# The second mixer's HGRN2 f and q projections move into the seven-product stage, with rope computed in PSUM and a new order around it

## The chip, the cores and the metric

The kernel runs on one core of one Trainium2 chip. What counts is the device time of one execution in microseconds (us). The same outputs are computed before and after; a run of the kernel before and one of the changed kernel can be compared on the same chip.

The engines are named as the profile names them: PE is TensorE (matmuls; PEld is its weight load), DVE is VectorE, ACT is ScalarE, POOL is GpSimd, SP is SyncE, whose queue issues every DMA of this kernel, in order. Matmuls write to PSUM, 8 banks of 128 x 512 float32 values here. DVE and ACT read PSUM and SBUF; POOL works on SBUF alone.

## The reference

A decoder trunk of two layers over 1024 tokens of width 1024. Layer 0 has another mixer (gated DeltaNet and short convolutions), which the change doesn't touch. Layer 1 has the mixer below, and each layer ends with a SwiGLU feed-forward network. Of the mixer's input projection, `hq` and `hf` are 4 heads of 128 columns each (HGRN2), `hi` and `hg` the values and gates of these heads, `sq`, `sk` and `sv` the queries, keys and values of 3 patterns x 4 heads of windowed attention.

```python
D_MODEL, SEQ, DEPTH, BATCH = 1024, 1024, 2, 1
SWA_PATTERNS = ((128, 1), (512, 4), (2048, 16))
...
def rope(x, pos):
    ...
    return jnp.concatenate([x1 * cos - x2 * sin, x1 * sin + x2 * cos], axis=-1).astype(x.dtype)
...
def hgrn2_recurrence(q, k, v, log_f):
    '''S_t = diag(f_t) S_{t-1} + k_t v_t^T with k_t = 1 - f_t, o_t = S_t^T q_t, chunkwise.
    q, k, log_f: (B, T, H, dk); v: (B, T, H, dv).'''
...
def mixer_cd(h, w_in, lower_bound, norm_g, w_out):
    ...
    hq, hf, hi, hg, sq, sk, sv = split_cols(h @ w_in, CD_SPLITS)
    lb = lower_bound.astype(f32)
    hf = hf.astype(f32)
    f_gate = lb + (1.0 - lb) * jax.nn.sigmoid(hf)
    log_f = jnp.log(f_gate)
    k_in = (1.0 - lb) * jax.nn.sigmoid(-hf)
    ...
    o_c = hgrn2_recurrence(hgrn_heads(jax.nn.silu(hq), HG_DK), hgrn_heads(k_in, HG_DK),
                           hgrn_heads(hi, HG_DV), hgrn_heads(log_f, HG_DK))
    o_c = (rms_norm(o_c, norm_g) * jax.nn.sigmoid(hgrn_heads(hg, HG_DV).astype(f32))).reshape(b, t, HG_VW)
    ...
    sq = rope(sq.reshape(b, t, n_pat, SWA_HEADS, SWA_DH), pos)
    sk = rope(sk.reshape(b, t, n_pat, SWA_HEADS, SWA_DH), pos)
    ...
    for p, (window, dilation) in enumerate(SWA_PATTERNS):
        o_p, lse_p = dilated_window_attention(sq[:, :, p], sk[:, :, p], sv[:, :, p], window, dilation)
        outs.append(o_p)
        lses.append(lse_p)
    wts = jax.nn.softmax(jnp.stack(lses, axis=-1), axis=-1)
    o_d = jnp.einsum('bthpd,bthp->bthd', jnp.stack(outs, axis=3), wts).reshape(b, t, SWA_HEADS * SWA_DH)
    return jnp.concatenate([o_c.astype(h.dtype), o_d.astype(h.dtype)], axis=-1) @ w_out
```

## The kernel before

Every matmul with a weight is done three times: weights and activations are split into a high part that the fast matmul format holds exactly and a low rest (`split`, lines 102 and 103: a cast on ACT, then a subtraction on DVE), and `mm3` (lines 127 to 129) adds high x high, high x low and low x high into one PSUM bank.

The second mixer's projections run in two stages.

The seven-product stage is the class `Local`, a subclass of the feed-forward network's `Up`. It handles two 128-column weight blocks at once, a pair `f` ("g" and "u"). The activations are four blocks (two halves of the tokens x two halves of the 1024 input channels), `b11`, `b21`, `b12`, `b22`, and the two weight blocks have two halves each. The four output blocks come from seven products of 4 x 3 matmuls instead of eight: p1, p2, p5, p6, p7 and the two that `end21` and `end12` add. The weights are combined first (`sums`, `sums_late` on POOL) and split in four parts: `part_a` (a11 and a12), `part_b` (s2 and s1, of the combined tile `ws`), `part_c` (s3 and a22) and `part_d` (s4, half a tile). The activations' combinations t1 to t4 are made once, in `turn`, which also works on the pairs 0 to 2; `pair` (line 862) does pair `f` and finishes pair `f - 1`. PE's order within `pair` is p1, p2, end21 of the pair before, end12 of the pair before, p6, p5, p7. Before the change the stage has 12 pairs: the queries and keys of pattern 1, then 2, then 0 (`PATTERNS`), 4 heads each.

All 12 get rope (line 766). A finished block lies in SBUF (`c`, `gt`, `u`) or, for one of four, in the PSUM bank `psu`. ACT copies its two 64-row halves, exchanged, to `sw` (lines 774 and 775), POOL multiplies `sw` by the sine table, DVE multiplies the block by the cosine table (line 779), and a later call adds the two into `z` (line 787), which is stored to DRAM (`qk`). The order on PE, DVE, ACT, POOL and SP in this stage is the order of the code (`manual_schedule`): each engine works its list from the top and waits where something isn't ready.

The rest of the mixer is `mixer_cd`. Here a framework's scheduler orders the instructions by priority, and each engine again works a fixed list. The projections of HGRN2's f and q (`hgrn_fq`, 2 weights x 2 halves x 8 x 3 matmuls for a head), the values (`hgrn_v`, `swa_v`) and the gates (`hgrn_gates`) run on PE one after another, and after each piece `tick` adds credit for two interleaved programs: the chain of 8 recurrence units (`hgrn`, 4 heads x 2 halves: exponentials, a reciprocal, a logarithm, a scan, seven levels of decayed blocks, state update, norm) and the attention of 12 heads (`Attend`). DVE splits the weights and does most of the two programs' elementwise work. What attention is left over at the end runs alone. Then `out_proj` loads the 8 finished blocks of `cat` and projects them.

The order of the projections is written out by hand at the end of `mixer_cd`: f and q of head 0 with the values of heads 0 and 1, the values of pattern 1, f and q of heads 1 and 2, the values of heads 2 and 3, the values of patterns 2 and 0, f and q of head 3, the gates. Attention of a pattern may start after its values.

PSUM is three groups of banks: `psu` (3), `psm` (3), `psg` (2). The weight ring has 2 raw tiles (and a spare one in `Local`) and 4 split ones.

Of the kernel before, what the change touches and what calls it, by code (L numbers as in the profile page):

```python
# [9 lines left out]
F32 = mybir.dt.float32  # L10
# [8 lines left out]
P = 128  # L19
T_LEN = 1024  # L20
# [11 lines left out]
PATTERNS = (1, 2, 0)  # L32
# [23 lines left out]
def hybrid_trunk_kernel(ctx: ExitStack, tc: tile.TileContext, x_t, w_all, w_down, w_ba, vecs, c_f, c_i, c_rope, out):  # L56
# [686 lines left out]
    class Local(Up):  # L743

        def __init__(self, left):
            self.left, self.n = left, 0
            self.qk = [dr.tile([2, P, T_LEN], F32, name=f"qk{f}") for f in range(12)]
            self.b12 = dr.tile([P, KH, HT], F32, name="b12")
            self.units = {f: {} for f in range(13)}
# [4 lines left out]
        def source(self, kind, f):  # L754
            p, h = PATTERNS[f // 4], f % 4
            return w_all[W_AT["cd", (16 if kind == "g" else 28) + p * 4 + h]]
# [8 lines left out]
        def block(self, name="c"):  # L765
            return self.right.tile([P, HT], F32, tag="c", name=name, bufs=3)

        def rope(self, f, i, half, c, src=None):

            src = c if src is None else src  # L770
            r = (None, 4, 16)[PATTERNS[f // 4]]
            t = slice(half * HT, (half + 1) * HT)
            sw = self.right.tile([P, HT], F32, tag="sw", name="sw", bufs=2)
            S.copy(sw[0:64], src[64:128])
            S.copy(sw[64:128], src[0:64])  # L775
            G.tensor_tensor(sw, sw, self.table[:, 1, t], op=MULT)  # L776
            self.flush()
            c = self.block() if c is None else c
            V.tensor_tensor(c, src, self.table[:, 0, t], op=MULT)

            def add():
                z = self.right.tile([P, HT], F32, tag="z", name="z", bufs=3)
                a, b, d = c, sw, z
                if r:
                    a, b = (y.rearrange("p (i r) -> p i r", r=r) for y in (a, b))
                    d = d.rearrange("p (r i) -> p i r", r=r)
                V.tensor_tensor(d, a, b, op=ADD)
                self.stores.append(lambda: dma(self.qk[f][i, :, t], z))

            self.adds.append(add)  # L790
# [7 lines left out]
        def rope11(self, f):  # L798
            self.rope(f, 0, 0, self.g1.pop(f))

        def rope22(self, f):
            self.rope(f, 1, 1, self.c22.pop(f))

        def add22(self, f):
            c = self.c22[f] = self.block()
            S.copy(c, self.x[f])  # L806
            V.tensor_tensor(c, c, self.z[f], op=ADD)
# [1744 lines left out]
```

## Time and profile before

| | us |
|---|---|
| median of 3 runs | 2614.49 |
| fastest and slowest of the 3 | 2611.93, 2616.2 |
| the profiled execution | 2614.26 |
| its span, first to last instruction | 2612.5 |

The table of the page's first part gives each engine's busy time as a share of the span. A matmul's record is longer (390 ns for 512 columns) than the distance to the next one (about 227 ns), since matmuls are pipelined: a stretch counts as busy even where the next matmul starts late by less than the difference, and the waits are better read from the view of waits and from the times at which matmuls start. In the view of waits each row names the waiting group, what it waited for, the sum in us, how often, and the longest. In the view of stretches the columns are the stretch, its length, the busy time of PE, PEld, DVE, ACT and POOL with their instruction counts, the granted TensorE clock, the DMA engines' share and GB/s.

The stretches that matter lie between about 1130 us (the last matmul of layer 0's down projection) and 1882 us (PE dense again in the output projection of the second mixer).

### The profile page before, as it was taken

The page shows a single profiled execution, that of the slowest core. Times are in us where ns is not written, and L with a number is a line of the kernel's source. Part 1 is how long each engine was busy: PE and PEld are TensorE (multiplying, and loading weights), DVE is VectorE, ACT ScalarE, POOL GpSimd, SP SyncE. Part 2 cuts the span into 40 slices and gives each one's busy share as a digit, 9 for nine tenths or more (in the row PEclk, how much of TensorE's full clock was granted, in tenths as well). Part 3 has the DMA queues.
Part 4 walks back from the last instruction along what each step waited for, and adds up shares of the span by engine and source line. Part 5 has one row for each costly group of instructions (what it writes and reads, how often), then busy time and mean ns, then how long its engine had stood idle before and what let it go on. Part 6 is the DMA issues. An engine that isn't in the chain of part 4 may idle for free. (4 is left out here: it accounts for less than half of the span.)

```text
span 2612.5 us, 37301 instructions
## 1 busy us (share of the span) xinstructions
PE 2539.2 (97%) x14005; PEld 2100.0 (80%) x14005; DVE 1742.7 (67%) x2877; ACT 1045.3 (40%) x1727; POOL 629.0 (24%) x541
## 2 busy tenths in 40 slices
PE   9999999999999999998999999999699999999998
PEld 7888888888888888876777879888587888888887
DVE  8887786775656665489777576558667665566554
ACT  5432113443333444344445354455444333334442
POOL 0111121342423200135553000000024433331001
PEclk9999999999999999998999999999899999999999
DMA  4435447235565797523324234464562455668853
GB/s 158 150 117 186 126 153 266 85 121 174 177 210 202 237 305 248 169 85 109 101 97 150 83 121 98 122 175 154 161 234 73 162 170 196 206 202 291 278 179 125
DMA packets 271957, 434.70 MB, mean 166 GB/s; under 512 B 48128, under 2 KB 136736, under 8 KB 271520
## 3 DMA queue, kind: packets, MB, share of 16 engines
q1 hardware_dynamic: 271776, 432.32, 50.6%
q8 instruction: 110, 1.80, 0.3%
q14 instruction: 71, 0.58, 0.1%
HBM read 296.35 MB, written 135.87 MB: 165 GB/s over the span
## 5 line engine op out<-in xcount | busy, mean ns | idle before, releaser
L103 DVE TENSOR_TENSOR w<-raw,w 128x1024 fp32r<-128x1024 f32 (+1 forms) x319 | 383.4, 1204 | 135.7 <-ACT w L102 135.0
L102 ACT CAST w<-raw 128x1024 fp32r<-128x1024 f32 (+1 forms) x319 | 306.8, 963 | 284.3 <-PE psu L129 143.2
L127 PE MATMUL psu<-hnh,w 128*128 128x512 f32 x880 | 352.2, 400 | 5.3 <-ACT w L102 5.3
L129 PE MATMUL psu<-hnh,w 128*128 128x512 f32 x880 | 345.9, 393 | 3.1 <-DVE w L103 3.0
L128 PE MATMUL psu<-hnl,w 128*128 128x512 f32 x880 | 344.8, 392 | 0.0
L188 POOL TENSOR_TENSOR acc<-acc,sq 128x512 f32<-128x512 f32 x52 | 77.2, 1485 | 525.2 <-ACT sq L184 459.6
L129 PEld LDWEIGHTS psu<-hnh,w 128*128 128x128 f32 x880 | 166.0, 189 | 41.7 <-DVE w L103 6.8
L127 PEld LDWEIGHTS psu<-hnh,w 128*128 128x128 f32 x880 | 166.4, 189 | 40.2 <-ACT w L102 6.1
L128 PEld LDWEIGHTS psu<-hnl,w 128*128 128x128 f32 x880 | 166.6, 189 | 33.0
L326 POOL TENSOR_TENSOR ws<-raw 128x512 f32<-128x512 f32 x50 | 69.7, 1395 | 370.6 <-DMA raw<-in_dram 226.5
L103 DVE TENSOR_TENSOR w<-ws,w 128x1024 fp32r<-128x1024 f32 x47 | 62.1, 1322 | 126.6 <-ACT w L102 126.6
L103 DVE TENSOR_TENSOR hidq<-hr,hidq 128x1024 fp32r<-128x1024 f32 x72 | 82.0, 1140 | 76.5 <-ACT hidq L102 76.1
L127 PE MATMUL psu<-t4h,w 128*128 128x512 f32 x224 | 90.9, 406 | 21.3 <-ACT c L806 20.8
L102 ACT CAST hidq<-hr 128x1024 fp32r<-128x1024 f32 x72 | 70.3, 980 | 101.3 <-DMA hr<-ts 61.2
L127 PE MATMUL psm<-hidq,w 128*128 128x512 f32 (+1 forms) x275 | 106.1, 386 | 0.0
L128 PE MATMUL psm<-hidq,w 128*128 128x512 f32 (+1 forms) x275 | 105.8, 385 | 0.0
L129 PE MATMUL psm<-hidq,w 128*128 128x512 f32 (+1 forms) x275 | 105.8, 385 | 0.0
L776 POOL TENSOR_TENSOR sw<-sw,rope 128x512 f32<-128x512 f32 x48 | 73.3, 1536 | 102.7 <-ACT sw L775 88.5
L417 POOL TENSOR_TENSOR hid<-hid,c 128x512 f32<-128x512 f32 x44 | 62.5, 1421 | 127.5 <-ACT hid L416 127.4
L128 PE MATMUL psu<-t4l,w 128*128 128x512 f32 x224 | 89.5, 400 | 0.0
L129 PE MATMUL psu<-t4h,w 128*128 128x512 f32 x224 | 89.2, 398 | 0.0
L127 PE MATMUL psu<-t3h,w 128*128 128x512 f32 x224 | 87.3, 390 | 0.0
(533 smaller groups left out, 6643.0 us busy)
## 6 DMA issues: line engine op xcount, KB each, us to landing
raw<-in_dram SPq DMA_DIRECT2D x227, 512.0 KB, 4.1
sd<-in_dram SPq DMA_DIRECT2D x44, 512.0 KB, 3.7
hid<-hid SPq DMA_DIRECT2D x88, 256.0 KB, 2.7
sd<-sd SPq DMA_DIRECT2D x44, 512.0 KB, 3.2
hr<-ts SPq DMA_DIRECT2D x40, 512.0 KB, 4.4
raw<-sd SPq DMA_DIRECT2D x40, 512.0 KB, 4.7
hd<-h SPq DMA_DIRECT2D x48, 256.0 KB, 2.2
h<-hd SPq DMA_DIRECT2D x48, 256.0 KB, 5.9
```

Of the source, the lines that this page charges most:

```text
L102: S.copy(hi, src)
L103: eng.tensor_tensor(lo, src, hi.bitcast(F32), op=SUB)
L127: T.matmul(o, lh, rh, start=first and i == 0, stop=False, **kw)
L128: T.matmul(o, lh, rl, start=False, stop=False, **kw)
L129: T.matmul(o, ll, rh, start=False, stop=last and i == n - 1, **kw)
L188: (eng or G).tensor_tensor(a, a, q, op=ADD)
L326: G.tensor_tensor(s[:, HT:], b[:, :HT], b[:, HT:], op=ADD)
L417: G.tensor_tensor(h, h, self.c22.pop(f), op=MULT)
L776: G.tensor_tensor(sw, sw, self.table[:, 1, t], op=MULT)
```

## The change

The number of pairs in `Local` goes from 12 to 16: HGRN2's f and q of head h become a pair (`PAIRS`, key `(None, h)`), ahead of the queries and keys of patterns 1, 2, 0. These four are not turned by rope; their blocks are stored to DRAM as they are, and `hgrn_fq` loads b and q of a unit from there, one unit ahead. The clamp and the silu, which read PSUM before, read SBUF now.

For the turned pairs the finished block now lies in PSUM in all four cases: `add11` adds into the bank of p2, `add12` into the bank of p5, `add22` into a new `psm` bank, and rope's multiplication by the cosine writes back to the same bank. `sw` has 3 buffers instead of 2.

The order within `pair` changes: `copy22` (the copy that reads `x[f - 1]`) is issued ahead of `part_b`; `part_b` and `sums_late` of a pair move from the end of the pair before to its beginning; `part_c` moves behind `end21`. The first weights of the stage are split in `early`, which runs outside the hand-written order, so that the scheduler may place it beside the down projection before, and the pool `hx` of layer 0's feed-forward network stays open for it.

In `mixer_cd` the values of pattern 1 and 2 follow the values of heads 0 and 1, then the values of heads 2 and 3, of pattern 0, and the gates; `tick` gives more credit per piece (2.1 and 1.7 instead of 1.75 and 1.25), caps both, and attention takes credit only while there is something to do. The output projection of this layer takes the blocks in the order 0, 1, 2, 4, 5, 6, 3, 7 (before: 4, 5, 6, 7, 0, 1, 2, 3); 0 to 3 are HGRN2's heads and 4 to 7 attention's.

```diff
-PATTERNS = (1, 2, 0)
+PAIRS = [(None, h) for h in range(4)] + [(p, h) for p in (1, 2, 0) for h in range(4)]
...
         def source(self, kind, f):
-            p, h = PATTERNS[f // 4], f % 4
-            return w_all[W_AT["cd", (16 if kind == "g" else 28) + p * 4 + h]]
+            p, h = PAIRS[f]
+            base = (4, 0) if p is None else (16 + p * 4, 28 + p * 4)
+            return w_all[W_AT["cd", base["gu".index(kind)] + h]]
...
+        def out(self, f, i, half, tile):
+            d = self.qk[PAIRS[f]][i, :, half * HT:(half + 1) * HT]
+            self.stores.append(lambda: dma(d, tile))
...
+        def turned(self, f):
+            return PAIRS[f][0] is not None
+
+        def rope(self, f, i, half, src):
...
+            sw = self.right.tile([P, HT], F32, tag="sw", name="sw", bufs=3)
+            S.copy(sw[0:64], src[64:128])
+            S.copy(sw[64:128], src[0:64])
+            G.tensor_tensor(sw, sw, self.table[:, 1, t], op=MULT)
+            self.flush()
+            V.tensor_tensor(src, src, self.table[:, 0, t], op=MULT)
+
+            def add():
+                z = self.right.tile([P, HT], F32, tag="z", name="z", bufs=3)
+                a, b, d = src, sw, z
...
+                V.tensor_tensor(d, a, b, op=ADD)
+                self.out(f, i, half, z)
...
+        def copy22(self, f):
+            c = self.c22[f] = self.right.tile([P, HT], F32, tag="c", name="c", bufs=2)
+            S.copy(c, self.x[f])
+
+        def add22(self, f):
+            c = self.c22.pop(f)
+            if self.turned(f):
+                b = self.c22[f] = psm()
+                V.tensor_tensor(b, c, self.z[f], op=ADD)
+            else:
+                V.tensor_tensor(c, c, self.z[f], op=ADD)
+                self.out(f, 1, 1, c)
...
+        def add11(self, f):
+            g, y = self.g1[f], self.y[f]
+            if self.turned(f):
+                V.tensor_tensor(y, y, g, op=ADD)
+            else:
+                V.tensor_tensor(g, g, self.y.pop(f), op=ADD)
+                self.out(f, 0, 0, g)
...
         def rope21(self, f):
             x = self.x.pop(f)
-            self.rope(f, 1, 0, None, x)
+            if self.turned(f):
+                self.rope(f, 1, 0, x)
+            else:
+                z = self.right.tile([P, HT], F32, tag="z", name="z", bufs=3)
+                S.copy(z, x)
+                self.out(f, 1, 0, z)
+                self.flush()
...
         def add12(self, f):
-            h = self.u2[f]
-            V.tensor_tensor(h, h, self.z.pop(f), op=ADD)
+            h, z = self.u2.pop(f), self.z[f]
+            if self.turned(f):
+                V.tensor_tensor(z, z, h, op=ADD)
...
         def pair(self, f, last, b11, b21, b22, t1, t2, t3, t4):
             n = f + 1
             self.p1(f, b11)
-            self.add22(f - 1)
+            self.copy22(f - 1)
             if not last:
                 an = self.raw("g", n, n % 3 == 1)
...
-            self.part_c(f, self.b)
-            self.rope22(f - 1)
+            self.add22(f - 1)
+            self.part_b(f, self.s)
+            self.sums_late(self.a, self.b, self.s)
             self.p2(f, b21, psm())
             g = self.snap(f)
-            if f in (3, 4):
-                self.rope11(2) if f == 3 else self.rope12(1)
+            self.rope22(f - 1)
             self.end21(f - 1, t4)
-            self.add11(f, g)
+            self.add11(f)
+            self.part_c(f, self.b)
             self.rope11(f)
             self.end12(f - 1, b22)
             self.rope21(f - 1)
...
             self.add12(f - 1)
             if not last:
                 self.part_a(n, an)
-            self.rope12(f - 1)
             self.p5(f, t1, psg())
-            if f == 3:
-                self.rope12(0)
+            self.rope12(f - 1)
             if not last:
-                s = self.sums(an, bn)
-                self.part_b(n, s)
-                self.sums_late(an, bn, s)
+                self.s = self.sums(an, bn)
...
+        def early(self, hx):
...
+            u0, g0 = (ring.tile([P, DM], F32, tag="raw", name="raw", bufs=2) for _ in range(2))
+            dma(g0, self.source("g", 0))
...
+            self.part_a(0, g0)
+            self.part_a(1, ga)
...
+            self.part_a(2, w2)
+            s = self.sums(g0, u0)
...
-            def hgrn_fq(h, w, tick, halves=range(NH)):
...
+            def hgrn_fq(h, half):
+                b, q = raws[h, half] = hl("b", bufs=2), hl("q", bufs=2)
+                for i, z in enumerate((b, q)):
+                    dma(z, qkd[None, h][i, :, half * HT:(half + 1) * HT])
 
             def hgrn(h, half, states):
-                b, q = raws[h, half]
+                if half + h == 0:
+                    hgrn_fq(0, 0)
+                b, q = raws.pop((h, half))
                 kk = hl("kk", bufs=2)
 
-                t = hl("t", bufs=1)
+                V.tensor_scalar(b, b, -44.0, None, op0=MAX)
+                t = hl("t", bufs=2)
                 S.activation(t, b, AF.Exp, scale=-1.0)
+                th = hl("t", bufs=2)
+                S.activation(th, q, AF.Tanh, scale=0.5)
+                V.scalar_tensor_tensor(q, th, 1.0, q, op0=ADD, op1=MULT)
+                if h * 2 + half < 7:
+                    hgrn_fq(*divmod(h * 2 + half + 1, 2))
...
-                credit[0] = min(credit[0] + 1.75 * cost, 3.0)
-                credit[1] += 1.25 * cost
-                while credit[0] >= 1 and have_c[0] * 2 > done_c[0]:
+                credit[0] = min(credit[0] + 2.1 * cost, 3.0)
+                credit[1] = min(credit[1] + 1.7 * cost, 3.0)
+                while credit[0] >= 1 and have_v[0] * 4 > done_c[0]:
...
-                while credit[1] >= 1:
+                while credit[1] >= 1 and (wanted or heads or busy[0]):
...
-            wv = hgrn_vw(0)
-            for half in range(NH):
-                hgrn_fq(0, wf, tick, (half,))
-                hgrn_v(0, wv, tick, range(half * 4, half * 4 + 4))
-                have_c[0] = have_v[0] = 1
+            hgrn_v(0, wv, tick, range(4))
+            have_v[0] = 1
+            hgrn_v(0, wv, tick, range(4, 8))
             swa_v(1, tick)
             attend(1)
-            fq(1)
-            fq(2)
+            swa_v(2, tick)
+            attend(2)
             hgrn_v(1, hgrn_vw(1), tick)
             have_v[0] = 2
-            swa_v(2, tick)
-            attend(2)
             swa_v(0, tick)
             attend(0)
-            fq(3)
             hgrn_gates(tick)
...
-                             (4, 5, 6, 7, 0, 1, 2, 3), half, hp)
+                             ((4, 5, 6, 7, 0, 1, 2, 3), (0, 1, 2, 4, 5, 6, 3, 7))[layer], half, hp)
```

174 lines of the change are left out of this document (74 added, 100 removed).

## The prediction

> **What bounds the kernel now.** I read the page's engine shares first, then a table of stretches cut at the stage's borders, then PE's rows in order of time at these borders, then what stands ahead of the waits.
>
> ```profile
> span 2612.5 us, 37301 instructions
> PE 2539.2 (97%) x14005; PEld 2100.0 (80%) x14005; DVE 1742.7 (67%) x2877; ACT 1045.3 (40%) x1727; POOL 629.0 (24%) x541
> ```
>
> PE is busy for 97% of the span, so time can come off in two ways: fewer matmuls, or PE waiting less. How far apart matmuls start when nothing is late shows in two rows with 63 matmuls of 512 columns from the one to the other: 14.30 / 63 = 0.227 us. The other rows are the stages' borders and waits.
>
> ```profile
> 1115.22 0.40 PE L129 MATMUL psu<-hidq,w 128*128 128x512 f32 x1
> 1129.52 0.39 PE L129 MATMUL psu<-hidq,w 128*128 128x512 f32 x1
> 1134.04 0.80 PE L127 MATMUL psu<-hnh,w 128*128 128x512 f32 x1 [4.13 <-ACT w L102]
> 1205.13 0.80 PE L127 MATMUL psu<-t4h,w 128*128 128x512 f32 x1 [7.63 <-ACT c L806]
> 1206.14 0.63 PE L129 MATMUL psu<-t4h,w 128*128 128x512 f32 x1
> 1206.57 0.63 PE L127 MATMUL psu<-t4h,w 128*128 128x512 f32 x1
> 1339.65 0.50 PE L127 MATMUL psu<-t4h,w 128*128 128x512 f32 x1 [1.44 <-ACT c L806]
> 1360.17 0.50 PE L127 MATMUL psu<-t4h,w 128*128 128x512 f32 x1 [1.10 <-ACT c L806]
> 1405.32 0.39 PE L128 MATMUL psu<-hnl,w 128*128 128x512 f32 x1
> 1755.31 0.48 PE L127 MATMUL psu<-hnh,w 128*128 128x512 f32 x1
> ```
>
> The seven-product stage runs from 1129.75 (0.227 behind the last row of the down projection) to 1405.32, where its last product has just ended: 275.6 us, less 0.9 for four matmuls of head 0's f that stand among them, 274.7. Its work is 12 pairs x 7 x 12 matmuls x 0.227 = 228.8 us. So 45.9 us are lost there, 3.8 a pair, and a pair costs 22.9 us. Outside the stage a pair of projections is 8 x 12 matmuls, 21.8 us. As it ran, the stage saved nothing over the plain form.
>
> ```profile
> PE psu L127 <- ACT c L806: 20.8, 9, 7.6
> PE psu L129 <- DVE w L103: 2.8, 5, 1.1
> PE psu L127 <- ACT w L102: 1.2, 1, 1.2
> ```
>
> The waits between 1180 and 1412 are nearly all one: `end21` waits for the copy `c` that `add22` makes, nine times, once for each pair 3 to 11. Behind the long ones PE is slow as well: after the 7.63 us wait matmuls start 0.43 us apart (1206.14 and 1206.57).
>
> ```profile
> 1129.70:1187.00 57.30, 51.48 (x229) 40.72 (x229) 53.03 (x51) 28.84 (x36) 23.22 (x11) 0.94 0.24 85
> 1405.50:1755.00 349.50, 343.81 (x3219) 294.71 (x3219) 211.05 (x546) 165.99 (x372) 21.36 (x40) 1.00 0.43 123
> 1755.00:1882.00 127.00, 105.52 (x993) 88.11 (x993) 101.20 (x327) 60.40 (x149) 6.77 (x11) 0.92 0.48 146
> 1200.00:1225.00 25.00, 19.68 (x74) 15.78 (x75) 22.09 (x21) 12.86 (x21) 11.94 (x9) 0.80 0.37 124
> 1339.65:1360.17 20.52, 19.43 (x84) 15.61 (x84) 14.99 (x16) 10.00 (x16) 12.43 (x9) 1.00 0.31 103
> 1550.00:1575.00 25.00, 22.21 (x332) 19.05 (x332) 20.94 (x62) 15.15 (x33) 2.52 (x6) 1.00 0.23 76
> 1775.00:1800.00 25.00, 24.45 (x140) 21.05 (x139) 21.17 (x68) 14.82 (x34) 1.74 (x4) 1.00 0.60 185
> 1338.07 1.04 ACT L102 CAST w<-ws 128x1024 fp32r<-128x1024 f32 x1 [4.96 <-POOL ws L327]
> 1339.02 0.58 ACT L806 COPY c<-psu 128x512 f32<-128x512 f32 x1
> ```
>
> The reader is to see three things. In the first pairs DVE is full (22.09 of 25 us from 1200 on, the clock at 0.80). In a late pair (1339.65 to 1360.17) no engine is: DVE 14.99, ACT 10.00, POOL 12.43 of 20.52. There the wait is one of order: the last two rows show ACT standing 4.96 us for POOL's `ws`, then casting it, and only then making the copy that PE waits for. And in the rest (1405.5 to 1755) PE is covered, 343.81 of 349.50, with DVE at 60%.
>
> **The change part by part.** *Matmuls.* Four heads of f and q leave the rest with 4 x 96 = 384 matmuls, of which 380 lie behind 1405.32: 86.3 us. They come back as 4 x 84: the stage's work becomes 16 x 84 x 0.227 = 305.1 us. On counts alone that is 48 matmuls, 10.9 us.
>
> *The stage's waits.* `copy22` now stands ahead of the cast of `ws`, and needs only p7 of the pair before, while `end21` comes two products (5.4 us) later. So the wait for `c` should go. What is late next? I lay a turned pair out on 19.07 us (84 x 0.227), with 2.72 us a product (12 x 0.227), 1.38 for an operation on POOL (12.43 / 9, above) and the two ACT rows just read; the positions are estimates from these. POOL's `sums` end about 2 us into the pair, the cast and subtraction of `part_b` by 4.5; p6, the first to need it, starts at 10.9. `sums_late` ends at about 5.5, `part_c` by 8; p7 starts at 16.3. Each has 6 us to spare. `part_a` is split by about 16.7 for the next p1 at 19.07: the smallest margin, 2 us.
>
> *DVE in a pair.* That only holds if DVE keeps up.
>
> ```profile
> L103 DVE TENSOR_TENSOR w<-raw,w 128x1024 fp32r<-128x1024 f32 x21 | 31.2, 1490 | 0.4 <-ACT w L102 0.4
> L103 DVE TENSOR_TENSOR w<-ws,w 128x1024 fp32r<-128x1024 f32 x9 | 11.5, 1275 | 28.9 <-ACT w L102 28.9
> L103 DVE TENSOR_TENSOR w<-raw,w 128x512 fp32r<-128x512 f32 x10 | 6.8, 676 | 0.0
> L787 DVE TENSOR_TENSOR z<-c,sw 128x512 f32<-128x512 f32 x24 | 27.0, 1126 | 2.6 <-POOL sw L776 2.3
> L787 DVE TENSOR_TENSOR z<-gt,sw 128x512 f32<-128x512 f32 x12 | 21.3, 1775 | 10.7 <-POOL sw L776 10.7
> L779 DVE TENSOR_TENSOR u<-u,rope x12: 691/1731/1775, 1223.0 to 1409.5; 128x512 f32<-128x512 f32 x12
> L779 DVE TENSOR_TENSOR c<-psu,rope x12: 665/678/696, 1188.5 to 1404.0; 128x512 f32<-128x512 f32 x12
> ```
>
> The last two rows (shortest, median, longest) are why in place matters: the same multiplication takes up to 1.775 us with both inputs in SBUF and never over 0.696 with one in PSUM. A turned pair has the four parts, 2 x 1.490 + 1.275 + 0.676 = 4.93 us; seven operations that now write PSUM (four multiplications, three additions); four additions into `z`. No row of before writes PSUM from DVE. From below I take 0.678 for each of the seven and of the four: 12.4 us. From above 1.775 for all: 24.4, which is over 19.07. I take 0.68 for the seven, since they differ from the 0.678 row only in the output, and 1.126 for the additions: 14.2 us, under 19.07 by 5.
>
> The Trainium skill ("PSUM — Partial Sum Buffer", Specifications) gives 1.04 ns per element for VectorE writing PSUM one element at a time; as an estimate from that page 512 elements are 0.53 us before any fixed part, so its sum would be the low one. No run here shows it yet.
>
> The unturned pairs need less: no multiplication, no `sw`, three additions and one copy on ACT. They are pairs 0 to 3, so the backlog of rope work behind the turn, which made the 7.63 us wait and the first slow pairs, has nothing to start from.
>
> *Longer held banks.* In-place rope keeps p2's bank until the addition in the same pair, p5's until about 5 us into the pair after next (its next writer comes at 13.6), x's until the end of the next pair (its next writer a pair later). Each ACT copy pair queues behind `snap` or a cast of about 1 us. I cost these at nothing; without the spare third bank a late addition would hold p1 by 1 to 3 us a pair.
>
> *`early`.* It takes the 4.13 us wait and the slow matmuls behind it off, if the scheduler's list, in which the three `part_a` splits stand before the down projection's last addition, gets its weights in time; SP must issue them between the saves of `hd`. I leave 0.5 us.
>
> The stage's losses after: 0.5 at the start, 2 for the turn's short matmuls and waits, 3 from the turn to pair 3 (DVE is nearly full in the turn, 53.03 of 57.30), 13 x 0.35 = 4.5 in the pairs: 10 us. The stage becomes 315.1, **+40.4**.
>
> *The rest, up to the gates' first matmul.* 349.5 - 86.3 = 263.2 us of the same mix. DVE loses 8 splits and the reads of PSUM:
>
> ```profile
> L103 DVE TENSOR_TENSOR w<-raw,w 128x1024 fp32r<-128x1024 f32 x30 | 36.7, 1224 | 29.4 <-ACT w L102 29.2
> L1844 DVE TENSOR_SCALAR b<-psu 128x512 f32<-128x512 f32 x8 | 5.5, 685 | 6.0 <-PE psu L129 6.0
> L1849 DVE SCALAR_TENSOR_TENSOR q<-q,psu 128x512 f32<-128x512 f32 x8 | 5.2, 656 | 4.3 <-ACT q L1847 4.3
> L1858 DVE TENSOR_SCALAR b<-t 128x512 f32<-128x512 f32 x8 | 3.4, 424 | 1.0 <-ACT t L1857 0.8
> L1860 DVE SCALAR_TENSOR_TENSOR kk<-t,omlb,b 128x512 f32<-128x512 f32 x8 | 6.0, 746 | 0.1
> ```
>
> 8 x 1.224 = 9.8, and 8 x (0.685 + 0.656 - 0.424 - 0.746) = 1.4. 211.05 - 11.2 = 199.9 us in 263.2: 76% instead of 60%. Where DVE stood at 84% before, PE idled for 11% (1550 to 1575) and 2% (1775 to 1800). At 76% I take 4%, 10.5 us, against 5.7 in the row: +6. The bounds are -4 and, at 11% all along, +23. The rest's part is **-80.3**. The new loads of b and q (as many bytes as the weights they replace) are asked for a unit ahead, on SP; the load of q waits for PE's last use of the same buffer, and stores of values and weight loads queue behind it. The upper bound of +23 holds that price too.
>
> *From the gates on.* DVE's list behind the first gate is 297 instructions, 298 before: the same work, 101.20 us of 127. PE's waits at the end are these:
>
> ```profile
> 1861.42 0.79 PE L127 MATMUL psg<-hnh,w 128*128 128x512 f32 x1 [3.69 <-ACT hnh L102]
> 1872.72 1.12 PE L2219 MATMUL psu<-cf,ol 128*128 128x128 f32 x4 [6.57 <-DVE ol L2214]
> 1879.79 0.80 PE L127 MATMUL psg<-hnh,w 128*128 128x512 f32 x1 [5.95 <-ACT hnh L102]
> ```
>
> With the blocks taken as they get ready, 43 matmuls of the output projection stand before the last combination of attention in PE's list, 20 before: 23 x 0.227 = 5.2 us of the 16 are filled. I take **-4**, between -12 (nearly all) and +10 (the denser DVE list stretches the stretch by 8%).
>
> Sum: +40.4 - 80.3 - 4 = -43.9. The profiled execution took 2614.3 (span 2612.5 and 1.8 around it; the median of the runs is 2614.5, the same within 0.01%): **2570 us**.
>
> **The rivals.** *A new wait in each pair.* The pairs keep what the late ones lose now, 20.52 - 19.07 = 1.45 instead of 0.35: 14.4 more, 2585. For it: margins of 2 us on in-order queues. Against: no engine over 75% of a pair.
>
> *The rest is uncovered.* PE idles for 11%, as from 1550 to 1575: 17 more than taken, 2587; with the +10 at the end 2601. For it: the chain of 8 units must run in 87 us less. Against: 96% and more of PE at DVE's 85%.
>
> *It doesn't do what it says.* The waits come back elsewhere, and only the 48 matmuls stay: 2603.
>
> *Slower.* DVE pays the SBUF price for what it writes to PSUM, and binds the stage: at 24.4 us a turned pair, 12 x (24.4 - 19.07) = 64 more, 2634. It decides from 43.9 / 12 = 3.7 us over 19.07, a pair of 22.7 us: with the additions at 1.775, from 1.52 us per write. For it: no row shows such a write, and the old stage did run at 22.9 a pair. Against: the PSUM read beside it is never slowed.
>
> **How the numbers follow.** Forecast 0.52 (2555 to 2582), new wait in the pairs 0.14, rest uncovered 0.14, only the count 0.07, slower 0.10, and 0.03 for a mixture that ends within 0.2%, 5 us, about what a measurement of this kernel can tell from no change. Faster is then 0.87, same 0.03, slower 0.10. With all terms at their good ends (losses 5 us less, -4, -12) the sum is -67, so the range begins at 2548; above, it takes in the uncovered rest and the mere count: 2605.
>
> **What would show it.** Right: no waits for the copy of `copy22` in the stage; pairs that start 19.1 to 19.5 us apart; DVE operations that write PSUM at about 0.68 us; the stage some 40 us longer and the stretch up to the gates some 80 shorter; no wait of 4 us ahead of the stage's first matmul. Wrong: DVE over 19 us a pair; new rows of waits for `psm` or `psu` banks; PE under 93% between the stage and the gates; SP held at a load of q with weights late behind it.

## The result and the profile after

The changed kernel takes 2567.5 us (median of 4 runs, 2565.6 to 2568.7) against 2614.1 before: a ratio of 0.9821, with a 95% interval of 0.9804 to 0.9838. That is 46.6 us less; 2570 was forecast. The profiled execution has a span of 2564.6 us, 47.9 below that of before. The page of the changed kernel begins:

```profile
span 2564.6 us, 37340 instructions
PE 2521.0 (98%) x13957; PEld 2089.1 (81%) x13957; DVE 1721.1 (67%) x2897; ACT 1058.4 (41%) x1751; POOL 644.0 (25%) x557
```

There are 48 matmuls less (14005 before), as counted. PE's rows in order of time give the borders of the stretches: the first product of the stage, the first products of the pairs 3, 4 and 15, the first matmul behind the stage's last product, the first gate, and the first product of the feed-forward network that follows.

```profile
1130.57 0.39 PE L127 MATMUL psu<-hnh,w 128*128 128x512 f32 x1
1188.15 0.39 PE L127 MATMUL psu<-hnh,w 128*128 128x512 f32 x1
1207.19 0.39 PE L127 MATMUL psu<-hnh,w 128*128 128x512 f32 x1
1416.63 0.39 PE L127 MATMUL psu<-hnh,w 128*128 128x512 f32 x1
1443.80 0.28 PE L127 MATMUL psu<-w,hnh 128*128 128x256 f32 x1
1710.74 0.48 PE L127 MATMUL psu<-hnh,w 128*128 128x512 f32 x1
1938.54 0.39 PE L127 MATMUL psm<-t1h,w 128*128 128x512 f32 x1
```

The last of these rows in the kernel before is this one:

```profile
1986.34 0.39 PE L127 MATMUL psm<-t1h,w 128*128 128x512 f32 x1
```

| stretch | before, us | after, us | difference | forecast |
|---|---|---|---|---|
| seven-product stage | 275.6 | 313.2 | +37.7 | +40.4 |
| from there to the first gate | 350.0 | 266.9 | -83.1 | -80.3 |
| from the gates to the next stage | 231.0 | 227.8 | -3.2 | -4 |

The stage also begins 0.8 us later, and what follows is the same (626.2 and 626.1 us). So the whole difference is in these three rows.

In the stage the written pairs start 19.04 us apart: from pair 4 to pair 15 the rows give (1416.63 - 1207.19) / 11 = 19.04. That is 84 matmuls at 0.227 us, so no time is lost there. The view of waits of PE from 1180 to 1450 is empty but for two rows at the border to the values:

```profile
PE psu L128 <- DVE w L103: 1.0, 1, 1.0
PE psu L127 <- ACT w L102: 0.4, 1, 0.4
```

The stretches (length, then PE, PEld, DVE, ACT, POOL, the clock, DMA share and GB/s) are four turned pairs and the two stretches of the rest:

```profile
1302.39:1378.55 76.16, 76.16 (x337) 63.06 (x336) 51.19 (x60) 40.40 (x60) 44.74 (x33) 1.00 0.31 111
1443.80:1710.74 266.94, 260.00 (x2833) 224.31 (x2832) 198.30 (x535) 158.14 (x367) 26.62 (x40) 0.99 0.54 155
1710.74:1938.54 227.80, 210.10 (x1467) 172.83 (x1466) 167.69 (x408) 100.39 (x199) 39.34 (x33) 0.96 0.54 174
```

DVE works 12.8 us of a turned pair (51.19 / 4), POOL 11.2. The groups of DVE in the written pairs 4 to 14 show what writing to PSUM costs (count, then busy time in us and mean ns of one):

```profile
L799 DVE TENSOR_TENSOR z<-psm,sw 128x512 f32<-128x512 f32 x21 | 21.4, 1018 | 2.1 <-POOL sw L789 1.3
L791 DVE TENSOR_TENSOR psm<-psm,rope 128x512 f32<-128x512 f32 x21 | 15.4, 732 | 2.0 <-ACT sw L788 1.9
L826 DVE TENSOR_TENSOR psm<-psm,gt 128x512 f32<-128x512 f32 x11 | 7.7, 700 | 4.5 <-PE psm L129 4.5
L812 DVE TENSOR_TENSOR psm<-c,psg 128x512 f32<-128x512 f32 x10 | 7.0, 696 | 17.7 <-ACT c L806 17.7
```

A multiplication in place takes 0.73 us and an addition 0.70, near the forecast's 0.68; the additions into `z` take 1.02, near its 1.126.

The size came out; it remains to see which part of the change took the waits away. The forecast put the late pairs' waits down to the place of `copy22` and those of the first pairs to a backlog of rope work that the unturned pairs don't make; rope in PSUM it counted as a cost and a risk.

### The profile page after: what moved, and what is told of

Its sections match the earlier page's. It is cut to its first block, busy times and chain, and to the rows that moved or that the text cites. A ratio compares the mean times of both kernels' runs of the same rounds, so it can differ in the third digit from the quotient of the medians.

```text
span 2564.6 us, 37340 instructions
## 1 busy us (share of the span) xinstructions
PE 2521.0 (98%) x13957; PEld 2089.1 (81%) x13957; DVE 1721.1 (67%) x2897; ACT 1058.4 (41%) x1751; POOL 644.0 (25%) x557
## 4 chain that ended last, share of the span: by engine, by line
PE 79%; DVE 10%; DMA 3%; ACT 2%; issue 2%; POOL 1%; SPq 0%; DVEq 0%; POOLq 0%; ACTq 0%
PE psu L127 14%; PE psu L129 14%; PE psu L128 14%; PE psg L127 6%; PE psg L129 6%; PE psg L128 6%; PE psm L127 4%; PE psm L128 4%; PE psm L129 4%; DVE w L103 1%; DVE h L249 1%; DMA raw<-in_dram 1%; DMA cm<-scr_o 1%; PE psm L2199 1%; DVE h L616 1%
## 5 line engine op out<-in xcount | busy, mean ns | idle before, releaser
L103 DVE TENSOR_TENSOR w<-raw,w 128x1024 fp32r<-128x1024 f32 x323 | 384.5, 1192 | 154.9 <-ACT w L102 154.4
L102 ACT CAST w<-raw 128x1024 fp32r<-128x1024 f32 x323 | 309.2, 959 | 254.6 <-PE psu L129 114.2
L127 PE MATMUL psu<-hnh,w 128*128 128x512 f32 x832 | 332.6, 400 | 0.0
L129 PE MATMUL psu<-hnh,w 128*128 128x512 f32 x832 | 326.0, 392 | 0.0
L128 PE MATMUL psu<-hnl,w 128*128 128x512 f32 x832 | 325.7, 392 | 0.0
L129 PEld LDWEIGHTS psu<-hnh,w 128*128 128x128 f32 x832 | 156.9, 189 | 33.5
L127 PEld LDWEIGHTS psu<-hnh,w 128*128 128x128 f32 x832 | 157.2, 189 | 32.4 <-issue 0.8
L128 PEld LDWEIGHTS psu<-hnl,w 128*128 128x128 f32 x832 | 157.2, 189 | 31.0
L127 PE MATMUL psu<-t4h,w 128*128 128x512 f32 x240 | 93.6, 390 | 0.5 <-ACT c L396 0.5
L129 PE MATMUL psu<-t4h,w 128*128 128x512 f32 x240 | 93.4, 389 | 0.0
L127 PE MATMUL psu<-t3h,w 128*128 128x512 f32 x240 | 93.4, 389 | 0.0
L128 PE MATMUL psu<-t3l,w 128*128 128x512 f32 x240 | 93.4, 389 | 0.0
L129 PE MATMUL psu<-t3h,w 128*128 128x512 f32 x240 | 93.4, 389 | 0.0
```

Of the source, the lines that this page charges most:

```text
L102: S.copy(hi, src)
L103: eng.tensor_tensor(lo, src, hi.bitcast(F32), op=SUB)
L127: T.matmul(o, lh, rh, start=first and i == 0, stop=False, **kw)
L128: T.matmul(o, lh, rl, start=False, stop=False, **kw)
L129: T.matmul(o, ll, rh, start=False, stop=last and i == n - 1, **kw)
```

## The experiments

All times are medians of 4 to 10 runs, each beside runs of the kernel before on the same chip (medians 2612.5 to 2614.2 us). The experiments ran on four chips, so the last column can be off by the 1.7 us between these medians; the ratio is free of that.

| run | us | ratio to before, 95% | against the changed kernel's 2567.5 |
|---|---|---|---|
| e1, order within the pair back | 2566.5 | 0.9822 (0.9805 to 0.9838) | -1.1 |
| e2, before with the new order in the pair | 2610.3 | 0.9986 (0.9977 to 0.9995) | +42.8 |
| e3, rope in SBUF | 2581.5 | 0.9875 (0.9860 to 0.9890) | +14.0 |
| e4, three extra DVE passes | 2609.5 | 0.9981 (0.9972 to 0.9991) | +42.0 |
| e5, e3 with turned pairs first | 2593.3 | 0.9918 (0.9901 to 0.9934) | +25.7 |
| e6, `early` in the written order | 2567.4 | 0.9823 (0.9809 to 0.9838) | -0.2 |
| e7, the rest's three orders back | 2589.0 | 0.9906 (0.9891 to 0.9921) | +21.4 |
| e8, one extra DVE pass | 2568.8 | 0.9828 (0.9813 to 0.9843) | +1.2 |
| e9, output projection's order back | 2565.0 | 0.9823 (0.9806 to 0.9839) | -2.6 |
| e10, credits back | 2578.0 | 0.9866 (0.9852 to 0.9881) | +10.5 |
| e11, credits up | 2561.6 | 0.9806 (0.9791 to 0.9820) | -6.0 |
| e12, order of the values back | 2559.7 | 0.9792 (0.9775 to 0.9808) | -7.9 |

### The order within the pair: e1 and e2

e1 puts `part_b` and `sums_late` back to the end of the pair before, so that ACT meets the cast of `ws` ahead of the copy that `end21` needs. The diffs here and below show the main lines only.

```diff
             self.add22(f - 1)
-            self.part_b(f, self.s)
-            self.sums_late(self.a, self.b, self.s)
             self.p2(f, b21, psm())
...
-                self.s = self.sums(an, bn)
+                s = self.sums(an, bn)
+                self.part_b(n, s)
+                self.sums_late(an, bn, s)
```

> The changed kernel, but part_b and sums_late of a pair stand again at the end of the pair before, so that the copy that end21 needs is behind the cast of ws on ACT. Theory A (the order took the waits away): end21's wait for c comes back, 0.5 to 1.4 us in each of the 13 written pairs, as in the late pairs of before: 6 to 18 us more, 2574 to 2586. Rival B (rope in PSUM and its lighter DVE took them away): no wait, 2565 to 2570.

e2 gives the kernel before the new order within a pair and nothing else.

```diff
-            self.add22(f - 1)
+            c = self.c22[f - 1] = self.block()
+            S.copy(c, self.x[f - 1])
...
-            self.part_c(f, self.b)
-            self.rope22(f - 1)
+            V.tensor_tensor(c, c, self.z[f - 1], op=ADD)
+            self.part_b(f, self.s)
+            self.sums_late(self.a, self.b, self.s)
             self.p2(f, b21, psm())
             g = self.snap(f)
+            self.rope22(f - 1)
...
             self.add11(f, g)
+            self.part_c(f, self.b)
```

> The kernel before with 12 turned pairs and rope in SBUF, and only the order within a pair changed: the copy of x ahead of part_b, part_b and sums_late at the beginning of the pair, part_c behind end21. Theory A: most of the 45.9 us lost in the stage goes, 25 to 35 us, 2579 to 2589; what stays is the start of the stage and the first pairs. Rival B: DVE stays full in the first pairs (22 of 25 us) and the waits move to another place: less than 10 us gained, 2604 to 2614.

Both went against theory A. e1 is not slower, and its pairs stay 19.04 us apart. e2 gains 3.9 us. Its first written pair, and a late one, as stretches:

```profile
1191.09:1220.11 29.02, 21.91 (x85) 17.25 (x84) 27.57 (x24) 13.63 (x21) 17.62 (x12) 0.88 0.32 109
1306.64:1327.15 20.51, 19.65 (x86) 15.61 (x84) 17.32 (x17) 10.28 (x16) 12.98 (x8) 1.00 0.29 103
```

DVE is full in the first (27.57 of 29.02 us), and a late pair takes 20.51 us as in the kernel before (20.52), though the copy now stands ahead of the cast. The late pairs no longer wait for `c`; from 1250 to 1400 us PE waits for the low parts `w` that DVE makes (3.3 us in five waits) and for `u` (0.4) instead, and once, at the end of the stage, 3.7 us for a cast. PE's rows show the waits of the first pairs at other places as well:

```profile
1201.23 0.80 PE L127 MATMUL psu<-t4h,w 128*128 128x512 f32 x1 [4.54 <-ACT c L860]
1242.47 0.80 PE L127 MATMUL psu<-t3h,w 128*128 128x512 f32 x1 [4.95 <-ACT u L389]
```

The row that named `c` in the profile of before told where PE stood, not why.

### Rope in SBUF or in PSUM: e3

e3 keeps the 16 pairs and the new order; rope's multiplication and the three additions of a turned pair write to SBUF as before. With this `sw` goes back to 2 buffers and `c` to 3, which the diff below leaves out.

```diff
-            V.tensor_tensor(src, src, self.table[:, 0, t], op=MULT)
+            c = self.block() if c is None else c
+            V.tensor_tensor(c, src, self.table[:, 0, t], op=MULT)
...
-                V.tensor_tensor(y, y, g, op=ADD)
+                V.tensor_tensor(g, g, y, op=ADD)
...
-                V.tensor_tensor(z, z, h, op=ADD)
+                V.tensor_tensor(h, h, z, op=ADD)
```

> The changed kernel with all 16 pairs and its order, but rope's multiplication and the three additions write to SBUF as before. Theory A: in place buys only slack: DVE in a turned pair rises from 12.8 to some 15 of 19.04 us, pairs stay 19.04 to 19.2 apart, 2565 to 2571. Rival B: the pairs lose over 1 us each, 12 of them: 2580 or more.

The time is rival B's: 14.0 us more. The count of pairs is not. Pairs 3 to 7 still take 19.04 us each, though 4 to 7 are turned, and only pairs 8 to 14 take 19.5 to 20.6: 7.7 us in all. In the profiles the stage is 16.7 us longer (329.9 against 313.2 us); the other 9 lie behind the start of pair 15 and are looked at below. Four of the slow pairs of e3 as a stretch, and then the groups of DVE and POOL in it:

```profile
1322.70:1403.90 81.20, 78.31 (x338) 62.48 (x336) 68.57 (x62) 40.50 (x61) 52.63 (x32) 1.00 0.28 94
```

```profile
L804 DVE TENSOR_TENSOR z<-u,sw 128x512 f32<-128x512 f32 x4 | 8.9, 2224 | 0.0
L804 DVE TENSOR_TENSOR z<-gt,sw 128x512 f32<-128x512 f32 x4 | 7.3, 1825 | 0.4
L796 DVE TENSOR_TENSOR gt<-gt,rope 128x512 f32<-128x512 f32 x4 | 7.0, 1740 | 0.0
L796 DVE TENSOR_TENSOR c<-c,rope 128x512 f32<-128x512 f32 x4 | 6.9, 1724 | 0.0
...
L793 POOL TENSOR_TENSOR sw<-sw,rope 128x512 f32<-128x512 f32 x16 | 27.6, 1722 | 27.6 <-ACT sw L792 27.6
```

The same group of POOL in four turned pairs of the changed kernel:

```profile
L789 POOL TENSOR_TENSOR sw<-sw,rope 128x512 f32<-128x512 f32 x16 | 20.7, 1295 | 31.1 <-ACT sw L788 31.1
```

The reader is to see that both engines get slower at once. DVE's multiplication takes 1.72 to 1.74 us with both inputs in SBUF against 0.73 in PSUM, and POOL's, which the change doesn't touch, takes 1.72 against 1.30. SBUF alone isn't the reason: the shortest of these multiplications with both inputs in SBUF takes 0.67 us (first to third number: shortest, median, longest, over the whole of e3):

```profile
L796 DVE TENSOR_TENSOR u<-u,rope x12: 673/1736/1780, 1243.0 to 1464.2; 128x512 f32<-128x512 f32 x12
```

DVE works 17.1 us a pair (68.57 / 4) instead of 12.8, POOL 13.2 instead of 11.2. The Trainium skill ("SBUF — State Buffer", Who interferes with whom) says that a DVE instruction with two SBUF inputs contends with a GpSimd instruction that reads SBUF, and one with at most one such input doesn't; these rows agree with it.

17.1 us is still under 19.04. Why pairs then take 20.3 on average (81.20 / 4) is seen in the rows in order of time of one such pair, where each engine waits for the next:

```profile
1363.80 0.62 ACT L791 COPY sw<-u 64x512 f32<-64x512 f32 x1 [2.15 <-DVE u L863]
1365.12 1.77 POOL L793 TENSOR_TENSOR sw<-sw,rope 128x512 f32<-128x512 f32 x1 [4.11 <-ACT sw L792]
1370.11 1.05 ACT L102 CAST w<-ws 128x1024 fp32r<-128x1024 f32 x1 [4.46 <-POOL ws L327]
1371.20 1.23 DVE L103 TENSOR_TENSOR w<-ws,w 128x1024 fp32r<-128x1024 f32 x1 [3.16 <-ACT w L102]
```

DVE's addition lets ACT make `sw`, POOL multiplies it and then makes `ws`, ACT casts that, DVE subtracts, and behind the subtraction stand the slow operations that delay the next addition. Three queues that work in order pass one pair's work around, and this round takes longer than the matmuls. That the round sets 20.3 us is read from these waits; no run lengthened one hand-over alone. The third buffer of `sw`, which e3 takes away as well, is a rival: ACT waits for a buffer once in most of the slow pairs (5.1 us in six waits from 1280 to 1425). But in the pair above DVE works without a gap from 1371.20 on past that place, and PE's waits for `u`, which ACT copies behind it, sum to 0.6 us.

At the end of the stage another wait comes out. These are DVE's and PE's rows in e3, and PE's in the changed kernel:

```profile
1444.46 0.69 DVE L804 TENSOR_TENSOR z<-gt,sw 128x512 f32<-128x512 f32 x1 [4.97 <-DMA qk<-z]
1449.68 0.58 PE L127 MATMUL psu<-w,hnh 128*128 128x256 f32 x1 [6.17 <-ACT w L102]
```

```profile
1436.27 0.38 PE L127 MATMUL psu<-w,hnh 128*128 128x256 f32 x1 [0.44 <-ACT w L102]
```

In e3 SP issues the loads of the values' weights at 1437.21, right when a subtraction of DVE ends that frees their tile (1437.19), and the last stores of `qk` behind them. That is 13.5 us into pair 15; in the changed kernel it is 7.5 (1424.12 and 1424.10). DVE then waits for a store in both (4.97 and 6.08 us), and ACT's cast of the values' weights comes behind that; in the changed kernel all this passes while PE still has products to do. So rope in SBUF costs time in two places: in the round of the slow pairs, and where a DVE that is late delays the stores.

### Where the turned pairs stand: e5

e5 is e3 with the pairs of pattern 1 first and HGRN2's behind them; the first three pairs' ropes stand where they stood before the change.

```diff
-PAIRS = [(None, h) for h in range(4)] + [(p, h) for p in (1, 2, 0) for h in range(4)]
+PAIRS = [(p, h) for p in (1, None, 2, 0) for h in range(4)]
```

> The kernel of e3 (16 pairs, rope in SBUF) with the pairs of pattern 1 first and HGRN2's four pairs behind them. Theory E (the unturned pairs at the beginning are what took away the slow first pairs): the first written pairs take 25 to 29 us again as before the change, and then HGRN2's four pairs 19.04 us: some 17 us over e3, 2595 to 2602. Rival F (where the turned pairs stand doesn't matter, their cost is the 1.4 us a pair of the late ones): 2578 to 2585 as e3.

11.8 us over e3, short of the 14 to 21 that theory E gave, and outside rival F's range. In the profiles the stage is 7.8 us longer than e3's (337.7 against 329.9 us); it also begins 2.8 us later, for which the edit gives no reason. The first written pair, and PE's wait in it:

```profile
1190.35:1218.91 28.56, 21.76 (x85) 17.15 (x84) 25.94 (x24) 13.64 (x21) 16.89 (x12) 0.88 0.28 102
```

```profile
1202.63 0.79 PE L127 MATMUL psu<-t4h,w 128*128 128x512 f32 x1 [6.68 <-ACT c L811]
```

28.6 us, then 22.1 and 20.6, 14.1 us lost in three pairs; then 19.04 for HGRN2's pairs and for the first turned ones behind them: the picture of before is back, the long wait and the low clock (0.88) too, and the unturned pairs drain it. That turned pairs 8 to 11 run at 19.04 here, and at 19.5 to 20.5 in e3, gives part of it back. Behind the turn, with its combinations of the activations, the rope work of three more pairs was what made DVE the bound. With rope in PSUM the place of the unturned pairs wasn't tried.

### How much room DVE has: e8 and e4

One, or three, passes over the block are added in each rope of a turned pair, in place in PSUM.

```diff
             self.flush()
+            V.tensor_scalar(src, src, 1.0, None, op0=MULT)
             V.tensor_tensor(src, src, self.table[:, 0, t], op=MULT)
```

> The changed kernel with one extra DVE pass (times 1.0, in place in PSUM) in each of the four ropes of a turned pair: some 2.9 us, DVE 12.8 + 2.9 = 15.7 of 19.04 us. Theory K (a margin of 2 us or more on every hand-over): pairs stay 19.04 to 19.2 apart, 2565 to 2570. Rival C (place in the queue counts): over 1 us a pair, 2580 or more.

> The changed kernel with three extra DVE passes over the block (times 1.0, in place in PSUM) in each of the four ropes of a turned pair: 12 x 0.73 = 8.8 us, DVE 12.8 + 8.8 = 21.6 us a pair. Theory A (only DVE's sum a pair counts): pairs 21.6 us apart, 12 x 2.6 = 31 more, 2598. Rival C (the place in the queue counts, not the sum: the passes hold part_a and the banks): more than that, pairs of 23 us and over, 2615 or more. Rival D (DVE writes to PSUM overlap something and cost less): 2580 or less.

With one pass nothing moves, as theory K said: this is a turned pair of e8, DVE at 15.45 of 19.04 us.

```profile
1301.33:1320.37 19.04, 19.04 (x86) 15.77 (x84) 15.45 (x19) 10.10 (x15) 11.18 (x9) 1.00 0.34 117
```

With three passes the time lies between theories A and C. Five late pairs of e4:

```profile
1309.19:1424.75 115.56, 102.15 (x422) 82.39 (x420) 105.96 (x141) 49.73 (x75) 55.77 (x40) 0.94 0.27 91
```

A pair is 23.1 us on average (20.5 to 25.6), and DVE works 21.2 of it (105.96 / 5): the sum of DVE explains most. The other 2 us go with waits and a lower clock (0.94), which no run separates. The passes took 0.70 to 0.76 us each (means), as rope's multiplication does, so rival D falls.

### The start: e6

```diff
-            self.early(hx)
...
             with tc.manual_schedule(engines=engines):
+                self.early(hx)
                 b22, t3, t4 = self.turn(tr, row, b11, b21, hx, close, left, right)
```

> The changed kernel, but early runs inside the hand-written order again, behind the down projection on PE, DVE, ACT and POOL. Theory G: the first product of the stage waits 4 to 5 us again, and matmuls behind it run slowly: 4 to 7 us more, 2571 to 2575. Rival H: the scheduler's freedom only moved DVE work that the down projection then waits for, 2565 to 2569.

No difference that 4 runs can tell (2564.8 to 2570.3). PE's rows of e6 show the last matmul of the down projection, the stage's first right behind it, and the first product of pair 2:

```profile
1131.62 0.39 PE L129 MATMUL psu<-hidq,w 128*128 128x512 f32 x1
1131.85 0.39 PE L127 MATMUL psu<-hnh,w 128*128 128x512 f32 x1
1144.51 0.48 PE L127 MATMUL psu<-hnh,w 128*128 128x512 f32 x1
```

The wait of 4.13 us is gone here too. Slow matmuls do come back: from the stage's first product to pair 3 it is 59.8 us (1131.85 to 1191.68) against 57.6, and the total doesn't show it. e6 keeps what else the change did at this place (the load of `g0` first, `part_a` ahead of the combinations, SP outside the written order); which of them did it wasn't tried.

### The rest: e7, e10, e9, e12, e11

Behind the stage, e7 puts back the credits, the order of the values and the output projection's order; e10, e12 and e9 put back one of them each, and e11 raises the credits.

```diff
-                credit[0] = min(credit[0] + 2.1 * cost, 3.0)
-                credit[1] = min(credit[1] + 1.7 * cost, 3.0)
+                credit[0] = min(credit[0] + 1.75 * cost, 3.0)
+                credit[1] = min(credit[1] + 1.25 * cost, 3.0)
...
-            swa_v(2, tick)
-            attend(2)
             hgrn_v(1, hgrn_vw(1), tick)
             have_v[0] = 2
+            swa_v(2, tick)
+            attend(2)
...
-                             ((4, 5, 6, 7, 0, 1, 2, 3), (0, 1, 2, 4, 5, 6, 3, 7))[layer], half, hp)
+                             ((4, 5, 6, 7, 0, 1, 2, 3), (4, 5, 6, 7, 0, 1, 2, 3))[layer], half, hp)
```

> The changed kernel, but in the rest the order of the values (heads 0 and 1, pattern 1, heads 2 and 3, pattern 2, pattern 0), the credit per piece (1.75 and 1.25) and the output projection's order (4 to 7, then 0 to 3) are as before the change. Theory I (the new order keeps PE covered though 380 matmuls of cover are gone): 8 to 20 us more, 2575 to 2588. Rival J (the units and attention are covered in either order): 2564 to 2570.

> The changed kernel with 1.75 and 1.25 credit per piece instead of 2.1 and 1.7. Theory M (with fewer pieces each has to carry more of the units and of attention, else they are left for the end): 8 to 18 us more, 2575 to 2586. Theory L: under 5 us, 2565 to 2572.

> The changed kernel, only the output projection of the second mixer takes its blocks in the order of before (4 to 7, then 0 to 3). Theory L (the tail's cover is the order by readiness): most of the 21.4 us that e7 lost, 10 to 20 us more, 2577 to 2588, with waits for hnh and for the last combination at the end. Rival M (the tail is short because the credit brings attention to an end earlier): under 5 us, 2565 to 2572. The prediction put the order's worth at 4 us.

> The changed kernel, only the values of heads 2 and 3 stand again ahead of those of pattern 2, so that the attention of pattern 2 may start later. e7 put back three things and lost 21.4 us; the credit alone is 10.5 of it and the output projection's order nothing. Theory O (the order of the values carries the rest by itself): 9 to 14 us more, 2576 to 2582. Rival Q (the three only cost together: attention left over at the end meets an output projection that starts with it): under 4 us, 2564 to 2571.

> The changed kernel with 2.5 and 2.0 credit per piece. From 1540 to 1710 us DVE works 113 of 170 us while PE is full, and behind 1710 PE idles for 15 of 130: if work of the units and attention that the end waits for can be pulled into the middle (theory M), 3 to 10 us less, 2557 to 2564. If it is held there by the values or by DVE's own chain (rival N): 2565 to 2575.

e7 loses 21.4 us, a little over theory I's upper end, and its waits from 1780 to 1960 are those of the tail:

```profile
PE psg L127 <- ACT hnh L102: 13.6, 3, 6.2
PE psu L2258 <- DVE ol L2253: 11.4, 5, 6.1
```

In the changed kernel the same two are short:

```profile
PE psg L127 <- ACT hnh L102: 4.5, 1, 4.5
...
PE psu L2258 <- DVE ol L2253: 0.7, 1, 0.7
```

e10 shows that the credits are worth 10.5 us (theory M): in its profile the stretch up to the first gate is shorter than in the changed kernel (258.4 against 266.9 us), and the one behind it longer (250.3 against 227.8). And e9 shows that the output projection's order by itself is worth nothing that 4 runs can tell. e12 went a way that neither theory had: with the values of heads 2 and 3 early again the kernel is 7.9 us faster. The rows that time two things show what moved: the 8 scans of the recurrence units, and the transposes of the combined attention (shortest, median, longest; first and last start). First the changed kernel, then e12:

```profile
L1901 DVE TENSOR_TENSOR_SCAN b<-rmask,t x8: 1216/1224/1227, 1458.0 to 1716.9; 128x512 f32<-128x512 f32 x8
...
L2258 PE MATMUL psu<-cf,ol x32: 270/272/475, 1742.3 to 1836.3; 128*128 128x128 f32 x32
```

```profile
L1901 DVE TENSOR_TENSOR_SCAN b<-rmask,t x8: 1218/1225/1225, 1458.6 to 1663.4; 128x512 f32<-128x512 f32 x8
...
L2258 PE MATMUL psu<-cf,ol x32: 272/273/474, 1758.4 to 1830.3; 128*128 128x128 f32 x32
```

The last scan starts at 1716.9 in the changed kernel and at 1663.4 in e12. The sixth and the seventh scan show where they part, first of the changed kernel, then of e12:

```profile
1601.46 1.22 DVE L1901 TENSOR_TENSOR_SCAN b<-rmask,t 128x512 f32<-128x512 f32 x1
1671.90 1.23 DVE L1901 TENSOR_TENSOR_SCAN b<-rmask,t 128x512 f32<-128x512 f32 x1 [0.21 <-ACT t L1900]
```

```profile
1600.43 1.23 DVE L1901 TENSOR_TENSOR_SCAN b<-rmask,t 128x512 f32<-128x512 f32 x1 [1.35 <-ACT t L1900]
1619.34 1.23 DVE L1901 TENSOR_TENSOR_SCAN b<-rmask,t 128x512 f32<-128x512 f32 x1 [2.43 <-ACT t L1900]
```

Six units begin about as early in both. The matmuls of the values of heads 2 and 3 run from 1609 to 1640 us in the changed kernel and from 1529 to 1580 in e12; that the fifth and sixth unit, which use these values, hold up the seventh is likely, but no run shows it alone. DVE is used where it was idle, as the stretch from 1540 to 1710 shows, first of the changed kernel, then of e12:

```profile
1540.00:1710.00 170.00, 166.63 (x1780) 144.26 (x1779) 113.36 (x363) 100.16 (x273) 13.04 (x23) 0.99 0.59 158
```

```profile
1540.00:1710.00 170.00, 167.47 (x1880) 143.47 (x1875) 132.38 (x397) 105.16 (x269) 16.58 (x29) 1.00 0.56 149
```

In the profiles e12 takes 9.6 us more up to the first gate and 16.5 less behind it. With the lower credits the early values of heads 2 and 3 don't help: in e7 the last scan is early too (1673.2), but the last transpose starts at 1857.1, 20.8 us after the changed kernel's. There attention is the late one. So e7's 21.4 us are 10.5 of the credits and a part that only arises together; how it splits between the values and the output projection's order wasn't tried.

e11 gains 6.0 us, as theory M said, though its last scan is as late as the changed kernel's (1720.8): the scans alone don't decide. e12 and e11 are both faster than the changed kernel (all their runs lie below its fastest, 2565.6); measured against the kernel before on each chip they gain 6.8 and 4.3 us, and the intervals of the ratios overlap a little with the changed kernel's. Both edits in one kernel weren't run.

## Why the prediction was right, step by step

*The count*: 48 matmuls less, 10.9 us, as forecast.

*The stage's losses.* 45.9 us before, 10 forecast, 7.4 measured (313.2, less six matmuls of the values among it, 0.7, less 305.1). Their places differ: 5.8 us lie ahead of pair 3 (57.58 from the first product to 1188.15, less 228 x 0.227; 5.5 were forecast), 1.4 in the two waits at the end, and none in the 13 pairs, for which 4.5 were set aside.

*The reason given for it was wrong.* The step that failed: "`copy22` now stands ahead of the cast of `ws` ... So the wait for `c` should go", and before it "There the wait is one of order". e1 undoes this order and nothing comes back; e2 does it alone, the late pairs stop waiting for `c`, and their waits move to `w` and `u`: it gains 3.9 us. The stage's length in the profiles, less its matmuls, gives the losses as 45.9 us before, 31.9 in e5, 24.1 in e3 and 7.4 in the changed kernel. So 16.7 us went with rope in PSUM (14.0 in the medians), and 7.8 with the unturned pairs behind the turn (with rope in SBUF); this second reason the text had given. The first 14.0 weren't taken apart: some 4 are the wait ahead of the first product, and e2 puts some 4 on the order. The text had the row that decides, 1.775 us against 0.696, and used it for the cost of a DVE operation; that the same contention lengthens POOL's work, and with it the round through three queues, it left out, and the stores at the stage's end too. So in-place rope stood there as a risk with a rival of its own, and not as a gain.

*The rival "slower"* put the break-even at a pair of 22.7 us. e4 comes close to that point: late pairs of 23.1 us, behind faster first ones, and a kernel 4.7 us under its own before. The rival's condition didn't come: the writes cost 0.70 to 0.73 us, not 1.52.

*`early`*: the wait went, as forecast, but not by the scheduler's freedom that the text named (e6); that freedom takes off only slow matmuls, some 2 us in the profiles.

*The rest.* Against the 86.3 us of its 380 matmuls, the two stretches of the rest became 83.1 + 3.2 = 86.3 us shorter: no net cost, where +6 and -4 were forecast. (The +6 is 4.8 by the numbers that it was worked out from, 10.5 less 5.7.) The rival "the rest is uncovered" was a real one: with the three old orders it costs 21.4 us (e7), more than the rival's 17. The credit, which the sum didn't price, holds off 10.5 us of it by itself (e10). The -4 for the output projection's order is not shown: e9 is 2.6 us faster without it, within the spread of its runs. The order of the values, passed over in the sum, costs some 7 to 8 us.

So the total came out within 2.5 us in part by luck: each stretch's waits were bounded by what could be lost there, but the cause of the largest saving wasn't known.

## What to carry to other kernels

A view of waits names the last link of a round through several queues in order; before an order is changed for it, look at which operations in that round are slow, and whether they are slow only beside another engine's. Moving one operand of a DVE operation into PSUM sped up two engines at once here. When matmuls that covered other work are taken away, it can pay to raise the share of that work per remaining matmul (10.5 us here), and see which of the interleaved programs ends last before its inputs are put later.

## What was not expected of the hardware

A DVE operation that reads and writes the same PSUM bank costs little more than one that reads PSUM and writes SBUF: 0.70 to 0.73 us (means) against 0.68 (median) for 512 columns. POOL's multiplication of 512 columns, untouched by the edit, takes 1.72 us where rope's operations on DVE have two SBUF inputs and 1.30 where they have one.
